# An encoder layer on one core: where the last sums of w_down are sent off, and how long a block waits between its load and its rounding

## The chip, the cores and the metric

The kernel runs on one core of one Trainium2 chip. The metric is the device time of one execution in microseconds; the kernel before takes 1858.98 us in the median of three runs (1856.39 to 1862.3).

## The reference

One transformer-like layer on 512 tokens of width 2048, all in float32:

```
h = RMSNorm(x);  z = h @ w_in            # q, k, v (8 heads of 128) and u (1024)
a = chunked attention(q, k, v)           # relative-position bias, softmax
p = trailing means of u minus u, mixed per group
x = x + RMSNorm(concat(a, p) @ w_o)      # w_o: 2048 x 2048
h = RMSNorm(x)
y = (gelu(conv3(h @ w_up)[:5632]) * conv3(h @ w_up)[5632:]) @ w_down   # w_down: 5632 x 2048
x = x + RMSNorm(y)
```

## The kernel before

**Arithmetic.** Every matrix is split into a rounded part and a rest (`split`, L140 on ScalarE and L141 on VectorE: `hi` is the rounded copy, `lo = src - hi`). A product is three matmuls, hi·hi, hi·lo and lo·hi (`mm3`, L162, L164, L165), each 128x512 in one PSUM bank. Large products are done by a seven-product scheme on 2x2 blocks (numbered 1 to 7, "L" and "a11 ... a22" in the names), so it needs sums of weight blocks as well as blocks.

**Sums of weights in DRAM.** Those sums are made by the DMA engines: `sums_in_dram` (from L285) is a generator of 48 transfers of 1 MB. A `copy` writes a block to a DRAM tile (`wt..` for w_o, `t_108` to `t_115` for the first 1024 rows of w_down), an `add` accumulates another block onto it. 32 are for w_o, 16 for w_down: copy and add to sum 5 (t_108, t_109), sum 7 (t_110, t_111), sum 6 (t_112, t_113, copied from t_108, t_109) and sum 4 (t_114, t_115, copied from t_112, t_113). `more_sums(n)` sends off the next n of them. It is called at places written by hand: in the loop over v (7 times), among the q and k products (18), in the head loop (4), in `mid` (8 over its calls), after `pool_keep` (7), and in `wo_product` (4). As long as `more_sums.paced` is true, a transfer is issued by GpSimd behind a pair of one-column memsets (`pace`: L295 on VectorE behind the last `split`, then L296 on GpSimd), so that it starts when the program has come that far. In w_o it is false: there a copy goes onto SyncE's queue behind the last weight load (L304), an add onto GpSimd's with no pace (L308).

**w_o.** Products run in the order 1, 7, 2, 5, 6, 3, 4, each for two column blocks `cc`, each in four steps `q`. A step reads one weight tile of 0.5 MB (`wo_cc_q` in the order, `wo_q` in the trace): SyncE loads it (L152) into one of 5 `raw` buffers, `split` writes hi and lo into one of 4 pairs of buffers, TensorE uses it for 12 matmuls. I number these tiles from the first of product 7 as T0: eight a product, so T16 is the first of product 5, T21 its sixth, T32 the first of product 3, T40 the first of product 4. Outputs are collected by `copy_out` (L902, ScalarE) and `add_out` (L906, VectorE); after product 6 there are three additions of 128x2048 (L946, L948, L949); after products 3 and 4 a norm, then `x2` (L980), the transposes `xt` back (L995) and their split into `gT` (L143, L144), which the first up-projection (`up`) reads.

**Ready blocks.** In the steps of products 7 to 4 the generator `ready_blocks` (from L839) also prepares three unsummed blocks of w_down as six half blocks: load `rw` (L843, SyncE), wait for some steps, `split` into `rwh` and, in place, `rw`; a step later the stores `rw01h`/`rw01l` and so on (L850, SyncE). There is one buffer of each, so a load waits until the store of the half block before has landed. They are read much later, in the down-projection.

**Who orders what.** TensorE's order is the program's. The other engines' queues are put in order when the program is built, from the order of the code, the buffers and the builder's own estimate of when things are ready. Each queue then runs strictly in that order.

Of the kernel before, what the change touches and what calls it, by code (L numbers as in the profile page):

```python
# [45 lines left out]
def f32(ap):  # L46
    return ap.bitcast(F32)
# [34 lines left out]
def encoder_layer(ctx: ExitStack, tc: tile.TileContext, x, xT, vecs, rel, post_mix, post_ffn,  # L82
# [23 lines left out]
    def bank(name):  # L106
        return psum.tile([P, 512], F32, tag="ps", name=name)
# [30 lines left out]
    def split(hi, lo, src, scale=None):  # L138
        if scale is None:
            rounded = nc.scalar.activation(hi, src, AF.Copy)  # L140
            rest = nc.vector.tensor_sub(lo, src, f32(hi))  # L141
        else:
            rounded = nc.scalar.activation(hi, src, AF.Copy, scale=scale)  # L143
            rest = nc.vector.scalar_tensor_tensor(lo, src, scale, f32(hi), op0=ALU.mult, op1=ALU.subtract)  # L144
        split.last, split.rest = rounded.ins, rest.ins
        return rounded.ins
# [182 lines left out]
    def more_sums(n):  # L329
        for _ in range(n):  # L330
            next(sums_step, None)
# [20 lines left out]
    for kb in range(KD):  # L352
        i, o = divmod(kb, 8)
# [9 lines left out]
        for what in "qk":  # L363
            _, hi, lo = first[f"{what}0_{i}"]
# [14 lines left out]
    def v_steps(i, ps):  # L379
        for n, c in enumerate(VORDER[i]):  # L380
            w = weights.get(f"v{i}_{c}", 2 if (i, n) == (1, 0) else None)
            if not i:
                pairs.prefetch(3 - FIRST_PART + weights.used)
            for j in range(2):
                kb = 2 * c + j
                for t in range(NT):
                    mm3(ps[t], g_tokens(hT, kb, t), part(w, j), n == j == 0, n == 7 and j == 1)
                if j and not i:
                    pairs.prefetch(3 - FIRST_PART + weights.used)
                yield  # L390
# [107 lines left out]
    psv = [bank(f"v0_{t}") for t in range(NT)]  # L498
    sums_of_x = x_sums()
    for n, _ in enumerate(v_steps(0, psv)):  # L500
        if n in (1, 3, 5, 7, 9, 11, 13):
            more_sums(1)
        for _ in range(2):
            next(sums_of_x, None)
        if n == 9:
            for i, v in enumerate(differences):
                split(*(hT[i][:, :, at, :] for at in AT[1]), v)
            early_x.close()
            p0 = mixing_w.enter_context(tc.tile_pool(name="p0", bufs=1, reuse_waits="tile"))
# [103 lines left out]
    with tc.tile_pool(name="p1", bufs=2, reuse_waits="tile") as p1:  # L613
# [43 lines left out]
        def ready_head(h):  # L657
            v = state.pop(("z", h))
            with tc.issue_after(split.rest):
                nc.vector.tensor_mul(v, v, RR)  # L660
            pair = [p1.tile([P, 2, S], F32R, tag="qk" + p, bufs=1, name="qk" + p) for p in "hl"]
            split(*pair, v)
            state["qk", h] = [tuple(p[:, n, :] for p in pair) for n in range(2)]
            if h + 1 < HEADS:
                load_z(h + 1)
# [6 lines left out]
        def v_ready():  # L672
            vh, vl = state["v"]
            for t in range(NT):
                with tc.issue_after(split.last):
                    split(vh[:, t, :], vl[:, t, :], f32(vl)[:, t, :], rt[:, t:t + 1])

        def scores(h):
            (q, k), bias = state.pop(("qk", h)), state.pop(("bias", h))
            with tc.issue_after(split.rest):  # L680
                nc.vector.memset(bias[:CHUNK, S - CHUNK:], -1e30)
            products = [bank(f"s{h}_{t}") for t in range(1, NT)]
            products = [products[0][:, 256:], *products]
            for t in range(NT):
                m = max(2, t + 1) * P
                sl = slice(t * P, (t + 1) * P)
                mm3(products[t][:, :m], (q[0][:, sl], q[1][:, sl]), (k[0][:, :m], k[1][:, :m]), True, True)
            for t in range(NT):
                n, ps = (t + 1) * P, products[t]
                s = t512("s", bufs=4)  # L690
                nc.vector.scalar_tensor_tensor(s[:, :n], ps[:, :n], SCALE, bias[:, S - n:],
                                               op0=ALU.mult, op1=ALU.add)
                nm = p1.tile([P, 1], F32, tag="st", bufs=16, name="nm")
                nc.vector.tensor_reduce(nm, s[:, :n], axis=AX.X, op=ALU.max, negate=True)
                sm = p1.tile([P, 1], F32, tag="st", bufs=16, name="sm")
                nc.scalar.activation(s[:, :n], s[:, :n], AF.Exp, bias=nm, accum_out=sm)
                rs = p1.tile([P, 1], F32, tag="st", bufs=16, name="rs")
                nc.vector.reciprocal(rs, sm)
                nc.vector.tensor_scalar_mul(s[:, :n], s[:, :n], rs)
                state["p", h, t] = s  # L700
            if h + 1 < HEADS:
                load_bias(h + 1)

        def turn(h):
            probs = [state.pop(("p", h, t)) for t in range(NT)]
            pts = [bank(f"pt{h}_{k}") for k in range(3)]
            pts = [pts[0], pts[1][:, P:], pts[2][:, 2 * P:], pts[1][:, :P]]
            for k in (0, 1, 3, 2):
                for t in range(k, NT):
                    nc.tensor.transpose(pts[k][:, (t - k) * P:(t - k + 1) * P],  # L710
                                        probs[t][:, k * P:(k + 1) * P], ident)
            for k in range(NT):
                n, at = S - k * P, PT_AT[k] + k * P - PT_Q[k]
                split(pth[:, at:at + n], ptl[:, at:at + n], pts[k])

        def values(h):
            ps = bank(f"a{h}")
            d = slice((h % 4) * DH, (h % 4 + 1) * DH)
            for k in range(NT):
                sl = slice(PT_AT[k], PT_AT[k] + S - PT_Q[k])  # L720
                mm3(ps[:, PT_Q[k]:], part(state["v"], k, d), (pth[:, sl], ptl[:, sl]), k == 0, k == NT - 1)
            nc.scalar.activation(mix(h), ps, AF.Copy)
# [42 lines left out]
        def run(n):  # L765
            for _ in range(n):
                next(steps, None)

        v_load(0)
        for h in range(3):  # L770
            if not h:
                run(2)
                ready_head(0)
            run(1)
            scores(h)
            if h:
                more_sums(1)
            run(1)
            if h:
                values(h - 1)  # L780
                more_sums(1)
            run(1)
            ready_head(h + 1)
            run(1)
            turn(h)
            if not h:
                v_ready()
# [3 lines left out]
        def mid(h):  # L791
            def step():
                values(h)
                more_sums(2 if h in (3, 4) else 1)
                if h == 2:
                    scores(3)
                elif h + 2 < HEADS:
                    ready_head(h + 2)
                if h == 3:
                    v_load(1)  # L800
            return step
# [37 lines left out]
        def ready_blocks():  # L839
            for at, j in ready_parts:  # L840
                v, hi = (p2.tile([P, 1024], dt, tag=tag, name=tag) for tag, dt in (("rw", F32), ("rwh", F32R)))
                lo = v.bitcast(F32R)
                nc.sync.dma_start(v.rearrange("p (a b) -> p a b", a=2),  # L843
                                  first_block(at[0], at[1] - 1, 0)[:, 2 * j:2 * j + 2, :])
                for _ in range(4):
                    yield
                split(hi, lo, v)
                yield
                for dest, part_ in zip(ready_w[at], (hi, lo)):
                    nc.sync.dma_start(dest[:, 2 * j:2 * j + 2, :], f32(part_).rearrange("p (a b) -> p a b", a=2))  # L850
                for _ in range(2):
                    yield

        ready_steps = ready_blocks()

        def wo_product(i, cc, left, between=None):
            ps = [bank(f"m{i}{cc}{t}") for t in range(2)]
            if cc and i in (2, 5, 6, 3):
                more_sums(1)
            for q in range(4):  # L860
                w = weights.get(f"wo{i}_{cc}_{q}")
                for j in range(2):
                    kb = 2 * q + j
                    for t in range(2):
                        mm3(ps[t], tuple(v[:, kb, t * P:(t + 1) * P] for v in left), part(w, j), kb == 0, kb == 7)
                if i != 1:
                    next(ready_steps, None)
                if between:
                    between(q)
            return ps  # L870
# [877 lines left out]
```

## Time and profile before

| | |
|---|---|
| median of 3 runs | 1858.98 us (1856.39 to 1862.3) |
| the profiled execution's own time | 1859.2 us |
| its span, first to last instruction | 1857.4 us |
| TensorE (PE) busy | 1843.6 us, 99% of the span |
| VectorE (DVE), ScalarE (ACT), GpSimd (POOL) busy | 1540.8, 1082.3, 303.2 us |
| granted TensorE clock | 0.999 |
| v and q/k products | about 30 to 215 us |
| heads and u projections | about 215 to 390 us |
| w_o | about 390 to 550 us |
| up-projection, down-projection | about 550 to 1440, 1440 to 1857 us |

Times are microseconds from the start of the span. A row of the timeline gives start, duration, engine, line, operation, output<-inputs, and in brackets how long the engine had stood idle before it and whom it waited for. A row of the waits gives engine and line, whom it waited for, and then the total, the number and the longest of these waits. "SPq" is SyncE's queue of DMA issues; a DMA's "us to landing" counts from its issue to its last byte. A matmul's duration overlaps with its successor's, so gaps of TensorE are read from the distance of starts.

### The profile page before, as it was taken

What the parts mean: (1) busy time and instruction counts of PE and PEld (TensorE: products, weight loads), DVE (VectorE), ACT (ScalarE), POOL (GpSimd) and SP (SyncE); (2) the same over time, 40 slices, a digit from 0 to 9 for tenths busy, and PEclk for the clock granted to TensorE, in tenths of its full rate; (3) what the DMA queues carried; (4) which work ended last, traced back from release to release, by engine and by line L of the source; (5) the groups of instructions that cost most, each with busy time, mean ns of one, the idle gap of its engine ahead of it and who ended that gap; (6) DMA issues with size and microseconds to landing.
All of it is one profiled execution on the core that took longest, in us unless ns stands there. A gap on an engine that the chain in (4) does not pass through costs nothing.

```text
span 1857.4 us, 25457 instructions
## 1 busy us (share of the span) xinstructions
PE 1843.6 (99%) x9598; PEld 1584.8 (85%) x9598; DVE 1540.8 (83%) x1804; ACT 1082.3 (58%) x1376; POOL 303.2 (16%) x402
## 2 busy tenths in 40 slices
PE   9999999999999999999999999999999999999998
PEld 7888888888878888888888888888888888888886
DVE  6988777887698988888888888888887899899876
ACT  7654455456464666566666665656655655565553
POOL 3411000100000122212222122121121001111101
PEclk9999999999999999999999999999999999999999
DMA  8599978999994798988888888899888967777785
GB/s 319 174 318 297 320 232 236 267 255 331 348 328 144 186 213 195 208 210 195 203 198 206 209 199 198 204 206 202 200 176 293 363 220 175 193 210 178 176 229 159
DMA packets 139338, 426.01 MB, mean 229 GB/s; under 512 B 11920, under 2 KB 15376, under 8 KB 133520
## 3 DMA queue, kind: packets, MB, share of 16 engines
q0 software_dynamic: 54864, 173.56, 46.1%
q1 hardware_dynamic: 84352, 250.84, 38.4%
q8 instruction: 75, 1.23, 0.3%
q14 instruction: 47, 0.39, 0.1%
HBM read 370.35 MB, written 104.33 MB: 256 GB/s over the span
## 4 chain that ended last, share of the span: by engine, by line
PE 93%; DMA 3%; DVE 2%; ACT 1%; issue 1%; SPq 0%; DVEq 0%; POOL 0%; POOLq 0%; ACTq 0%
PE qa L170 18%; PE qa L176 10%; PE qg L170 9%; PE qg L176 5%; PE qd L170 4%; PE pa L164 4%; PE pa L165 4%; PE pa L162 4%; PE qd L176 2%; PE pg L164 2%; PE pg L165 2%; PE pg L162 2%; PE m L164 2%; PE m L165 2%; PE m L162 2%; PE v L164 2%
## 5 line engine op out<-in xcount | busy, mean ns | idle before, releaser
L140 ACT ACTIVATE wfh<-wx 128x1024 fp32r<-128x1024 f32 x192 | 203.4, 1059 | 152.7 <-PE qg L170 55.4
L170 PE MATMUL qa<-gT,wfh 128*128 128x512 f32 x1152 | 288.6, 392 | 0.0
L141 DVE TENSOR_TENSOR wfl<-wx,wfh 128x1024 fp32r<-128x1024 f32 x192 | 234.7, 1222 | 59.8 <-ACT wfh L140 44.8
L170 PEld LDWEIGHTS qa<-gT,wfh 128*128 128x128 f32 x1152 | 207.2, 189 | 37.1
L1365 POOL DMA_DIRECT2D wx<-in_w_up x122 | 104.7, 858 | 502.2 <-DVE wfl L141 473.8
L140 ACT ACTIVATE wfh<-wy 128x1024 fp32r<-128x1024 f32 x96 | 101.7, 1060 | 109.3 <-PE qg L170 57.9
L170 PE MATMUL qg<-h,wfh 128*128 128x512 f32 x656 | 162.2, 389 | 0.9 <-ACT zb L1421 0.9
L176 PE MATMUL qa<-gT,wfl 128*128 128x256 f32 x1152 | 161.2, 283 | 0.1
L176 PEld LDWEIGHTS qa<-gT,wfl 128*128 128x128 f32 x1152 | 151.6, 191 | 4.3 <-ACT zm L1425 0.3
L170 PEld LDWEIGHTS qg<-h,wfh 128*128 128x128 f32 x656 | 122.9, 188 | 26.7 <-ACT zb L1421 1.3
L141 DVE TENSOR_TENSOR bl<-b,bh 128x2048 fp32r<-128x2048 f32 x56 | 127.2, 2287 | 19.1 <-ACT bh L140 11.7
L140 ACT ACTIVATE bh<-b 128x2048 fp32r<-128x2048 f32 x56 | 106.1, 1913 | 55.1 <-DVE b L1129 22.8
L141 DVE TENSOR_TENSOR wfl<-wy,wfh 128x1024 fp32r<-128x1024 f32 x96 | 117.2, 1221 | 10.9 <-ACT wfh L140 6.4
L162 PE MATMUL pa<-bh,ah 128*128 128x512 f32 x320 | 124.5, 389 | 0.0
L164 PE MATMUL pa<-bl,ah 128*128 128x512 f32 x320 | 124.5, 389 | 0.0
L165 PE MATMUL pa<-bh,al 128*128 128x512 f32 x320 | 124.5, 389 | 0.0
L141 DVE TENSOR_TENSOR wfl<-wz,wfh 128x1024 fp32r<-128x1024 f32 x48 | 58.7, 1224 | 54.1 <-PE qa L170 54.1
L176 PEld LDWEIGHTS qg<-h,wfl 128*128 128x128 f32 x656 | 89.5, 190 | 6.4
L170 PE MATMUL qd<-gT,wfh 128*128 128x512 f32 x384 | 94.9, 389 | 0.0
L176 PE MATMUL qg<-h,wfl 128*128 128x256 f32 x656 | 91.5, 282 | 0.0
L170 PEld LDWEIGHTS qd<-gT,wfh 128*128 128x128 f32 x384 | 72.0, 188 | 14.9
L170 PE MATMUL qa<-h,wfh 128*128 128x512 f32 x328 | 82.1, 392 | 0.0
(550 smaller groups left out, 4363.5 us busy)
## 6 DMA issues: line engine op xcount, KB each, us to landing
wx<-in_w_up POOLq DMA_DIRECT2D x122, 512.0 KB, 6.1
b<-in_w_down SPq DMA_DIRECT2D x32, 1024.0 KB, 6.8
wt<-in_w_o POOLq DMA_DIRECT2D x24, 1024.0 KB, 15.8
wx<-in_w_up SPq DMA_DIRECT2D x43, 512.0 KB, 5.5
wz<-in_w_up SPq DMA_DIRECT2D x41, 512.0 KB, 6.0
wy<-in_w_up SPq DMA_DIRECT2D x41, 512.0 KB, 4.6
wy<-in_w_up POOLq DMA_DIRECT2D x41, 512.0 KB, 6.9
sum<-part POOLq DMA_DIRECT2D x38, 512.0 KB, 6.8
```

What stands on the lines that cost most here:

```text
L140: rounded = nc.scalar.activation(hi, src, AF.Copy)
L141: rest = nc.vector.tensor_sub(lo, src, f32(hi))
L162: nc.tensor.matmul(ps, l[0], r[0], start=first, stop=False, skip_group_check=onto)
L164: nc.tensor.matmul(low, l[0], r[1], start=False, stop=False, skip_group_check=onto)
L165: nc.tensor.matmul(ps, l[1], r[0], start=False, stop=last, skip_group_check=onto)
L170: nc.tensor.matmul(ps, w[0][:, kb], pairs[kb][0], start=fresh and not kb, stop=last, skip_group_check=not fresh)
L176: nc.tensor.matmul(ps[:, sl], w[1][:, kb], pair[:, sl], start=False, stop=last, skip_group_check=not fresh)
L1365: nc.gpsimd.dma_start(self.raw[k, what], self.block(k, m, kh), accum_op=ALU.add)
```

## The change

The number of transfers stays 48, and so does their order. Three calls of `more_sums` are added early and three are taken out of `wo_product`: the v loop calls it 8 times (also at its last step), the head loop also at head 0, `mid` twice also at head 5; `wo_product` calls it at product 5 only. The last four transfers, the copies and adds of sum 4, so become three paced ones and one in w_o. In `ready_blocks` five steps instead of four lie between load and split, and one instead of two behind the stores, so a half block still takes seven steps.

```diff
     for n, _ in enumerate(v_steps(0, psv)):
-        if n in (1, 3, 5, 7, 9, 11, 13):
+        if n % 2:
             more_sums(1)
...
             scores(h)
-            if h:
-                more_sums(1)
+            more_sums(1)
...
                 values(h)
-                more_sums(2 if h in (3, 4) else 1)
+                more_sums(2 if h in (3, 4, 5) else 1)
...
-                for _ in range(4):
+                for _ in range(5):
                     yield
                 split(hi, lo, v)
                 yield
                 for dest, part_ in zip(ready_w[at], (hi, lo)):
                     nc.sync.dma_start(dest[:, 2 * j:2 * j + 2, :], f32(part_).rearrange("p (a b) -> p a b", a=2))
-                for _ in range(2):
-                    yield
+                yield
...
-            if cc and i in (2, 5, 6, 3):
+            if cc and i == 5:
                 more_sums(1)
```

What this does to the queues shows at three places. The first is GpSimd's queue from the end of the heads to the first norm of w_o; `t_114` and `t_115` are sum 4, `small` is the norm's power. Before:

```order
L308 DMA t_112<-in_w_down 512x1x512
L296 MEMSET pace 128x1
L308 DMA t_113<-in_w_down 512x1x512
L308 DMA t_114<-in_w_down 512x1x512
L308 DMA t_115<-in_w_down 512x1x512
L967 TENSOR_TENSOR small<-small,mhalf 128x2 x2
```

In the change:

```order
L308 DMA t_113<-in_w_down 512x1x512
L296 MEMSET pace 128x1
L301 DMA t_114<-t_112 16x16384
L296 MEMSET pace 128x1
L301 DMA t_115<-t_113 16x16384
L308 DMA t_115<-in_w_down 512x1x512
L296 MEMSET pace 128x1
L308 DMA t_114<-in_w_down 512x1x512
L965 TENSOR_TENSOR small<-small,mhalf 128x2 x2
```

Both copies now stand in GpSimd's queue, paced, and the add onto t_115, though written in product 5, needs no pace and stands ahead of the last paced one.

The second is SyncE's queue in w_o from the second half block's store to the third and fourth loads; `wt_96` and `wt_97` hold the weights of product 5, `wo_0_1r` there is T17. Before:

```order
L850 DMA rw01l<-rw 128x1024
L152 DMA wo_0_1r<-wt_96 128x1024
L304 DMA t_114<-t_112 16x16384
L152 DMA wo_0_2r<-wt_96 128x1024
L152 DMA wo_0_3r<-wt_96 128x1024
L152 DMA wo_1_0r<-wt_97 128x1024
L843 DMA rw<-in_w_down 128x2x512
L152 DMA wo_1_1r<-wt_97 128x1024
L152 DMA wo_1_2r<-wt_97 128x1024
L152 DMA wo_1_3r<-wt_97 128x1024
L850 DMA rw11h<-rwh 128x1024
```

In the change:

```order
L849 DMA rw01l<-rw 128x1024
L152 DMA wo_0_1r<-wt_96 128x1024
L152 DMA wo_0_2r<-wt_96 128x1024
L842 DMA rw<-in_w_down 128x2x512
L152 DMA wo_0_3r<-wt_96 128x1024
L152 DMA wo_1_0r<-wt_97 128x1024
L849 DMA rw11h<-rwh 128x1024
L849 DMA rw11l<-rw 128x1024
L152 DMA wo_1_1r<-wt_97 128x1024
L152 DMA wo_1_2r<-wt_97 128x1024
L152 DMA wo_1_3r<-wt_97 128x1024
L842 DMA rw<-in_w_down 128x2x512
```

The copy is gone, the third load stands behind T18's instead of T20's, and the fourth, which before stood behind T27's, behind T23's: five tiles between the two loads instead of seven. The fifth moves from behind T34's to behind T30's, the sixth from behind T40's to behind T37's.

The third is ScalarE's queue in product 5; `wo_0_0h` there is T16, `wo_1_1h` T21, `junk` sums of squares. Before:

```order
L140 ACTIVATE wo_0_0h<-wo_0_0r 128x1024
L140 ACTIVATE wo_0_1h<-wo_0_1r 128x1024
L140 ACTIVATE wo_0_2h<-wo_0_2r 128x1024
L140 ACTIVATE rwh<-rw 128x1024
L140 ACTIVATE wo_0_3h<-wo_0_3r 128x1024
L910 ACTIVATE junk,small<-y_4299 128x1024
L140 ACTIVATE wo_1_0h<-wo_1_0r 128x1024
L910 ACTIVATE junk,small<-y_4299 128x1024
L140 ACTIVATE wo_1_1h<-wo_1_1r 128x1024
```

In the change:

```order
L140 ACTIVATE rwh<-rw 128x1024
L140 ACTIVATE wo_0_0h<-wo_0_0r 128x1024
L140 ACTIVATE wo_0_1h<-wo_0_1r 128x1024
L140 ACTIVATE wo_0_2h<-wo_0_2r 128x1024
L140 ACTIVATE wo_0_3h<-wo_0_3r 128x1024
L908 ACTIVATE junk,small<-y_4311 128x1024 x2
L140 ACTIVATE wo_1_0h<-wo_1_0r 128x1024
L140 ACTIVATE rwh<-rw 128x1024
L140 ACTIVATE wo_1_1h<-wo_1_1r 128x1024
```

The third rounding moves ahead of T16, and the fourth, which stood behind T25, ahead of T21; the fifth moves from behind T32 to behind T27, the sixth from behind T40 to behind T34. VectorE's subtractions `rw<-rw,rwh` move with them: the last one leaves its place among the tiles of product 4 and comes to stand in product 3, just ahead of T35.

## The prediction

> **What bounds the kernel now.** I read the page's first table, then TensorE's waits, then its starts one by one.
>
> ```profile
> span 1857.4 us, 25457 instructions
> PE 1843.6 (99%) x9598; PEld 1584.8 (85%) x9598; DVE 1540.8 (83%) x1804; ACT 1082.3 (58%) x1376; POOL 303.2 (16%) x402
> ```
>
> TensorE is busy 1843.6 of 1857.4 us, and the change leaves its instructions and their order as they are. So only its gaps can shrink, and a wait anywhere else matters only if it opens a new one. The waits of TensorE (engine and line, waited for, total, times, longest):
>
> ```profile
> PE up L162 <- DVE gT L144: 1.6, 1, 1.6
> PE up L164 <- DVE gT L144: 0.7, 2, 0.5
> PE m L164 <- DVE wo_1l L141: 0.3, 1, 0.3
> PE m L164 <- DVE wo_0l L141: 0.3, 1, 0.3
> ```
>
> All of these lie in w_o (`m`) or just behind it (`up` waits for `gT`); the few others are at the program's start and in the up-projection, which the change does not touch. The recorded idle time understates a gap, as the starts show:
>
> ```profile
> 509.61 0.39 PE L162 MATMUL m<-wo_3h,s 128*128 128x512 f32 x1
> 510.07 0.50 PE L164 MATMUL m<-wo_3l,s 128*128 128x512 f32 x1
> 512.74 0.39 PE L162 MATMUL m<-wo_0h,s 128*128 128x512 f32 x1
> 513.41 0.50 PE L164 MATMUL m<-wo_0l,s 128*128 128x512 f32 x1 [0.28 <-DVE wo_0l L141]
> 516.04 0.39 PE L162 MATMUL m<-wo_1h,s 128*128 128x512 f32 x1
> 516.75 0.50 PE L164 MATMUL m<-wo_1l,s 128*128 128x512 f32 x1 [0.32 <-DVE wo_1l L141]
> ```
>
> Undisturbed, starts are 0.23 us apart (two rows further down, 458.06 and 471.66, stand five tiles of 12 matmuls apart: 2.72 us a tile). These three steps take 0.46, 0.67 and 0.71, together 1.15 too long, and the late matmuls last 0.50 instead of 0.39, which holds up the next ones by 0.11 each: 1.5 us lost. With the 1.6 and the 0.7 above, w_o and its end hold 3.8 us that a better order could give back, 0.2% of the span. That caps the gain.
>
> Why VectorE is late with those tiles: first the chain of waits (start, duration, what), then ScalarE's timeline.
>
> ```profile
> 463.05 8.42 DMA rw11l<-rw
> 483.14 10.00 DMA rw11l<-rw
> ```
>
> ```profile
> 500.77 1.06 ACT L140 ACTIVATE rwh<-rw 128x1024 fp32r<-128x1024 f32 x1 [5.22 <-DMA rw<-in_w_down]
> ```
>
> A half block's load waits for the store before it, SyncE's queue waits with it, and ScalarE stands 5.22 us before a load that has not landed, with VectorE's subtraction behind it and the w_o tiles behind that. VectorE does not catch up before the norm. Transfers are slow there, since the DMA engines are full. The queues and issues of the window from 440 to 495 (for a queue packets, MB, share; for an issue count, KB, median us to landing):
>
> ```profile
> q1 hardware_dynamic: 4638, 17.08, 81.5%
> q0 software_dynamic: 1056, 2.10, 20.6%
> t<-in_w_down POOLq DMA_DIRECT2D x2, 1024.0 KB, 15.9
> rw<-in_w_down SPq DMA_DIRECT2D x3, 512.0 KB, 7.5
> rw11l<-rw SPq DMA_DIRECT2D x2, 512.0 KB, 9.2
> rw01l<-rw SPq DMA_DIRECT2D x1, 512.0 KB, 3.9
> ```
>
> The last two adds are all of q0's 20.6%, the two copies of 1 MB about a tenth of what q1 moved, so some 10%.
>
> **The change part by part.** *The four transfers leave w_o.* This frees about 30% of the DMA engines from 440 to 495 and two issues from SyncE's queue. The add written in product 5 stands in GpSimd's queue right behind a copy that is issued among the heads, so it goes early too.
>
> *The half blocks come closer together*, load to load 5 tiles (13.6 us at 2.72 a tile) instead of 7 for the third and fourth. With L for a load and S for a store of the rest:
>
> ```profile
> 434.45 0.37 SPq L843 DMA_DIRECT2D rw<-in_w_down  x1
> 440.43 1.06 ACT L140 ACTIVATE rwh<-rw 128x1024 fp32r<-128x1024 f32 x1 [2.81 <-issue]
> 442.78 0.32 SPq L850 DMA_DIRECT2D rw01l<-rw  x1
> 447.32 0.34 SPq L152 DMA_DIRECT2D wo_2r<-wt  x1
> 458.06 0.39 PE L164 MATMUL m<-wo_0l,n 128*128 128x512 f32 x1
> 471.66 0.39 PE L164 MATMUL m<-wo_1l,n 128*128 128x512 f32 x1
> ```
>
> The third load now follows T18's (447.32), so it goes at 448. Behind its landing come rounding (1.1), its subtraction (1.15) and the subtraction of T16, which now stands behind it (1.2): T16 is ready at 451.5 + L, and TensorE reads it at 458.06. The store goes at 448 + L + 2.3, the fourth load at 448 + L + 2.3 + S + 0.4, and T21, behind its rounding, is ready at 454.2 + 2L + S; TensorE reads it at 471.66. So T16 needs L up to 6.6, T21 needs 2L + S up to 17.5. The second load gives L = 6.0 (434.45 to 440.43). S was 3.9 as the first copy began, 9.2 beside copies and adds, and for the last two stores of the phase, from the page's list of DMA issues:
>
> ```profile
> rw02l<-rw SPq DMA_DIRECT2D x2, 512.0 KB, 5.9
> ```
>
> I take L = 6.0 and S from 3.9 to 5.9, the rows with fewer sums beside them: 2L + S is 15.9 to 17.9, T21 0 to 0.4 us late; I count 0.4. With 7.5 and 9.2 it is the rival A below. The fifth and sixth loads follow at seven tiles (19 us) each, and the cycle L + S + 2.7 is 14.6 at most: nothing.
>
> *What then happens at 500 to 570.* Without the 5.22 us for which the tiles stood behind a load, the three come in time: -1.5. And the norm's chain comes earlier:
>
> ```profile
> 526.82 1.22 DVE L141 TENSOR_TENSOR rw<-rw,rwh 128x1024 fp32r<-128x1024 f32 x1
> 527.96 0.68 DVE L906 TENSOR_TENSOR y<-m,y 128x512 f32<-128x512 f32 x1
> ```
>
> Product 3 ended on TensorE at 524.6 (471.66, 19 more tiles, the 1.5 lost, less a matmul). Its output is added 3.3 us later, since VectorE is behind and does the sixth `rw` (1.2) first. That one moves into product 3, and the backlog goes with the stall. The norm's chain runs on VectorE from there to `gT`; 3.3 us earlier there cover the 1.6 us wait even with TensorE 1.5 us earlier: -1.6. The two smaller waits for `gT` (0.7) hang on product 4's end, which moves up as TensorE does: counted at 0, at best -0.7.
>
> *Three more paced transfers among v and the heads.* Each costs VectorE a one-column memset in phases where TensorE waits for nothing, and GpSimd a memset and an issue, 0.8 us by the distance of two adds. GpSimd's only other work near them is the power for the first norm, which comes to stand behind the transfer added at the end of v:
>
> ```profile
> 77.43 1.82 POOL L308 DMA_DIRECT2D wt<-in_w_o  x1
> 78.22 2.32 POOL L308 DMA_DIRECT2D wt<-in_w_o  x1
> 79.99 1.63 POOL L218 TENSOR_TENSOR rt<-rt,mhalf 128x4 f32<-128x4 f32 x1
> 82.33 0.60 PE L223 MATMUL R<-ident,rt 128*128 128x128 f32 x4
> ```
>
> It ends at 81.62, TensorE needs it at 82.33: 0.7 us of cover for 0.8 of delay, so 0.1, dropped as rounding. The thin place is the end of the heads. The last paced slot is
>
> ```profile
> 386.26 1.16 POOL L308 DMA_DIRECT2D t<-in_w_down  x1
> ```
>
> and in the change the slots before it carry the two copies, and this one both last adds. Here the first w_o tiles are loaded (ScalarE, VectorE, TensorE; then the loads' time to landing in the window 380 to 420):
>
> ```profile
> 402.39 1.06 ACT L140 ACTIVATE wo_2h<-wo_2r 128x1024 fp32r<-128x1024 f32 x1 [4.68 <-DMA wo_2r<-in_w_o]
> 403.48 1.23 DVE L141 TENSOR_TENSOR wo_2l<-wo_2r,wo_2h 128x1024 fp32r<-128x1024 f32 x1 [2.01 <-ACT wo_2h L140]
> 406.38 0.39 PE L164 MATMUL m<-wo_2l,a 128*128 128x512 f32 x1
> ```
>
> ```profile
> wo_1r<-in_w_o SPq DMA_DIRECT2D x1, 512.0 KB, 15.0
> wo_2r<-in_w_o SPq DMA_DIRECT2D x1, 512.0 KB, 10.5
> ```
>
> This tile is ready at 404.71 and read at 406.38: 1.67 us of slack. Its load took 10.5 us while one add ran. The nearest row for a worse case is the tile before it, which took 15.0 us: 4.5 later, less 1.67, is +2.8. From below, two copies in place of two adds could bring it earlier, but no gap is there to close: 0. I take 0, since its load already ran beside an add all the way.
>
> A sentence of the Trainium skill bears on this: DMA: Bandwidth & Descriptors, "Queues, rings and completion order", says that each DMA engine goes round robin over the queues that have work, a packet at a time. By it a second add in GpSimd's queue keeps that queue busy for longer but takes no more than its half from SyncE's loads, so the price would be 0. No run here shows one add against two beside the same load.
>
> Sum: -1.5 - 1.6 + 0.4 = -2.7, on the profiled execution's own 1859.2 us (span 1857.4 and 1.8 around it), which stands 0.2 above the median of the runs: **1856.5 us**.
>
> **The rivals.** *A: the ready blocks become the wait.* If L and S stay as they were (7.5 and 9.2), because w_o's own loads fill the engines, T16 is 0.9 late and 2L + S = 24.2 puts T21 6.7 late in all. Against the -3.1 that is +3.6: 1862.8. It decides from 2L + S = 20.6. For it: three of the six half blocks now come sooner and stand further ahead of the tiles; against it: the 3.9 us store. *B: the heads pay.* The +2.8 above eats the gain: 1859.3. For it: 1.67 us of slack, and the same bytes moved to where the DMA engines are also busy; against it: TensorE waited for no tile there, although this load was among the slowest. The Trainium skill says on the same page, "Issuing engines are not separate DMA queues", that a transfer runs on the same 16 engines whichever queue issues it; the 15.0 us row agrees, and it is what B rests on. *C: the relief does nothing*, VectorE stays behind through its own work (the three 128x2048 additions): 1859.2. *A and B together*: 1862.8 + 2.8 = 1865.6.
>
> **How the numbers follow.** Forecast 0.50, B 0.18, C 0.09, A 0.17, A with B 0.06. The forecast's best, with the 0.7 and the 0.4 back, is 1855.4. Single runs of before lie from 1856.39 to 1862.3, 3 us to either side, so I put 2 us below that, 1853.5, and on top 1864.0, a little over A; A with B is left out. About 0.3% (5.6 us) is what a measurement of this kernel tells from no change. Faster by more, under 1853.4, needs more than the gaps hold: 0.05. Slower by more, over 1864.6, is A with B and A's upper part: 0.12. Within: 0.83.
>
> **What would show it.** Right: no TensorE wait for `wo_.l` between 500 and 520, `up` no longer waiting 1.6 us for `gT`, `rw11l` landing in under 6 us, and the third and fourth `rwh` waiting under 5 us for their loads. Wrong: gaps at T16 or T21 (near 458 and 471), which is A; a gap between 400 and 415, which is B; or both gaps at 510 and 550 as before, C.

## The result, and the profile after

The changed kernel takes 1866.97 us (median of 5 runs, 1865.08 to 1867.78), the kernel before 1858.49 beside it (1856.39 to 1862.3): a ratio of 1.0049, with a 95% interval from 1.0038 to 1.006. It is 8.5 us slower. The prediction was 1856.5 us, with a range up to 1864.0: the sign was wrong, and the time lies above the range. The profiled execution took 1866.97 us.

The first table of its page, and TensorE's waits up to 700 us, without those at the program's start and in the first projections (engine and line, waited for, total, times, longest):

```profile
span 1865.2 us, 25457 instructions
...
PE 1847.0 (99%) x9598; PEld 1586.2 (85%) x9598; DVE 1540.2 (83%) x1807; ACT 1082.6 (58%) x1376; POOL 304.4 (16%) x407
```

```profile
PE u L162 <- DVE ptl L141: 2.3, 1, 2.3
PE up L162 <- DVE gT L144: 2.0, 1, 2.0
PE m L164 <- DVE wo_0l L141: 1.3, 2, 0.9
...
PE R L223 <- POOL rt L218: 0.9, 1, 0.9
PE m L164 <- DVE wo_3l L141: 0.6, 1, 0.6
PE m L164 <- DVE wo_2l L141: 0.3, 1, 0.3
PE m L164 <- DVE wo_1l L141: 0.3, 1, 0.3
...
```

Two waits are new and lie far ahead of w_o: `u` for `ptl` (among the heads, near 318 us) and the `R` transposes for `rt` (near 82). Both waits in w_o that should have gone are there still: the late tiles (now four, T35 to T38, near 517 to 527) and `up` for `gT`, 2.0 instead of 1.6. A third is new in w_o, `wo_0l` at T16:

```profile
464.78 0.50 PE L164 MATMUL m<-wo_0l,n 128*128 128x512 f32 x1 [0.94 <-DVE wo_0l L141]
```

**The first new wait.** GpSimd's queue at the end of v, and TensorE's row behind it:

```profile
77.93 2.33 POOL L308 DMA_DIRECT2D wt<-in_w_o  x1
78.67 1.69 POOL L296 MEMSET pace<- 128x1 f32 x1
78.71 2.84 POOL L308 DMA_DIRECT2D wt<-in_w_o  x1
79.70 3.36 POOL L218 TENSOR_TENSOR rt<-rt,mhalf 128x4 f32<-128x4 f32 x1
```

```profile
83.11 0.65 PE L223 MATMUL R<-ident,rt 128*128 128x128 f32 x4 [0.91 <-POOL rt L218]
```

The power for the first norm ends at 83.06 instead of 81.62. The adds start 0.8 us apart, but they end at 80.26 and 81.55, 1.3 apart. What follows an add ends behind it, as the rows show: the memset between the two ends at 80.36, 0.1 us behind the first add, and the power 1.5 us behind the second (in the kernel before 1.1 us behind its last add).

**The second new wait.** ScalarE stands before the rounding of the second half of v, whose load `vl<-vd` has not landed:

```profile
314.08 2.56 ACT L143 ACTIVATE vh<-vl,rt 128x512 fp32r<-128x512 f32 x4 [7.12 <-DMA vl<-vd]
```

The same in the kernel before, then the DMA issues from 295 to 325 us of before and after (count, KB, median us to landing):

```profile
310.56 2.56 ACT L143 ACTIVATE vh<-vl,rt 128x512 fp32r<-128x512 f32 x4 [4.43 <-DMA vl<-vd]
```

```profile
t<-in_w_down POOLq DMA_DIRECT2D x2, 1024.0 KB, 18.4
wt<-in_w_o POOLq DMA_DIRECT2D x1, 1024.0 KB, 14.3
vl<-vd SPq DMA_DIRECT2D x1, 1024.0 KB, 6.8
```

```profile
t<-in_w_down POOLq DMA_DIRECT2D x3, 1024.0 KB, 16.8
vl<-vd SPq DMA_DIRECT2D x1, 1024.0 KB, 9.5
```

The load takes 9.5 us instead of 6.8. Everything behind it on ScalarE and VectorE comes later: `pth`, `ptl`, the rounding of `u_0`. There are as many transfers beside it as before, but with two calls added ahead of this place, others: the kernel before issues an add and two copies there, the changed one a copy and two adds.

**In w_o** the transfers do go. From 440 to 495 us only SyncE's queue is left, and loads and stores land faster (`rw` in 5.5 us instead of 7.5, `rw11l` in 5.8 instead of 9.2):

```profile
q1 hardware_dynamic: 5351, 16.80, 87.4%
rw<-in_w_down SPq DMA_DIRECT2D x4, 512.0 KB, 5.5
rw11l<-rw SPq DMA_DIRECT2D x2, 512.0 KB, 5.8
```

Yet ScalarE waits longer for the half blocks than before. Its third, fifth and sixth `rwh`:

```profile
461.27 1.06 ACT L140 ACTIVATE rwh<-rw 128x1024 fp32r<-128x1024 f32 x1 [6.87 <-issue]
...
494.02 1.06 ACT L140 ACTIVATE rwh<-rw 128x1024 fp32r<-128x1024 f32 x1 [6.02 <-DMA rw<-in_w_down]
...
513.92 1.06 ACT L140 ACTIVATE rwh<-rw 128x1024 fp32r<-128x1024 f32 x1 [7.29 <-DMA rw<-in_w_down]
```

VectorE's subtraction behind the fourth rounding (474.29) and SyncE's queue from there to the fifth load show why:

```profile
477.47 1.22 DVE L141 TENSOR_TENSOR rw<-rw,rwh 128x1024 fp32r<-128x1024 f32 x1
...
479.85 0.32 SPq L152 DMA_DIRECT2D wo_3r<-wt  x1
480.22 0.43 SPq L849 DMA_DIRECT2D rw11h<-rwh  x1
...
481.36 0.96 SPq L849 DMA_DIRECT2D rw11l<-rw  x1
...
489.87 0.38 SPq L842 DMA_DIRECT2D rw<-in_w_down  x1
```

The rest's store goes out 7.1 us after its rounding began, not the 2.3 that the two engines need. VectorE subtracts a weight tile first, T21, so the half block's subtraction ends 4.4 us behind the start of the rounding. Then the store stands 2.7 us in SyncE's queue, behind weight loads that wait for a free buffer. It lands 8.5 us later, the next load 4.2 after that: 19.7 us from rounding to rounding, and 19.9 to the one after. The seven tiles of a block give 19.0. So each half block comes 0.7 to 0.9 us later against its tiles, and the last one meets T35.

**The sum.** For each kernel I added up by how much two neighbouring starts in TensorE's timeline stand farther apart than undisturbed (0.227 us for a matmul of 512 columns, 0.120 for 256, others in proportion). It is one profiled execution each, a missing record adds 0.2, and fixed gaps such as those of transposes are in it too; so only differences of over half a microsecond in a cell are read. "w_o" is 400 to 600 us and ends with `up`. A stretch in which TensorE runs at half its clock (last section) adds about 1.5 us to a cell. Such a stretch lies in 300-340 of the change, of "no call at v's end" and of the change with held loads, in w_o of the change, of "no call at v's end" and of both kernels with late calls, and in 200-300 of both with sums in q, k. The time is the median, with the ratio to the kernel before on the same chip and its 95% interval; one execution of "sums in q, k (1)" that took 3747 us is left out, and so is one of the kernel before beside it, of 10581 us.

| kernel | 60-100 | 200-300 | 300-340 | 340-400 | w_o | us | ratio |
|---|---|---|---|---|---|---|---|
| before | 1.0 | 2.2 | 1.3 | 1.2 | 8.1 | 1858.5 | 1 |
| the change | 2.2 | 2.4 | 5.5 | 1.2 | 11.9 | 1867.0 | 1.0049 [1.0038, 1.006] |
| steps only | 1.1 | 2.2 | 1.6 | 1.2 | 8.0 | 1859.6 | 1.0007 [0.9994, 1.0019] |
| moves only | 2.1 | 2.4 | 3.7 | 2.2 | 10.0 | 1865.5 | 1.0039 [1.0025, 1.0053] |
| no call at v's end | 0.8 | 2.2 | 6.0 | 1.3 | 10.8 | 1866.2 | 1.0044 [1.0031, 1.0057] |
| late calls | 0.8 | 2.4 | 1.4 | 1.7 | 14.5 | 1866.3 | 1.0047 [1.0031, 1.0063] |
| left out | 1.0 | 2.2 | 1.4 | 1.2 | 9.1 | 1862.0 | 1.0012 [1.0002, 1.0022] |
| left out, loads held | 1.0 | 2.2 | 1.5 | 2.6 | 4.6 | 1856.0 | 0.9985 [0.9976, 0.9995] |
| before, loads held | 0.8 | 2.9 | 1.3 | 2.7 | 6.9 | 1858.4 | 1.0002 [0.9991, 1.0013] |
| the change, loads held | 2.3 | 2.4 | 5.3 | 1.4 | 4.3 | 1860.0 | 1.0007 [0.9997, 1.0016] |
| vl beside one copy | 1.8 | 2.2 | 3.1 | 1.2 | 12.6 | 1866.7 | 1.0037 [1.0023, 1.0051] |
| late calls, loads held | 0.8 | 2.4 | 1.3 | 1.2 | 11.7 | 1861.0 | 1.0011 [1.0001, 1.002] |
| no sum by vl, held | 2.0 | 2.4 | 1.3 | 1.2 | 8.6 | 1860.9 | 1.0011 [1.0002, 1.002] |
| and rt first | 0.8 | 2.5 | 1.3 | 1.2 | 7.8 | 1858.8 | 0.9996 [0.9986, 1.0006] |
| add first, held | 1.1 | 3.3 | 2.3 | 5.1 | 4.2 | 1862.2 | 1.0023 [1.0013, 1.0033] |
| sums in q, k (1) | 1.1 | 10.9 | 1.8 | 1.3 | 4.1 | 1864.3 | 1.004 [1.0027, 1.0052] |
| sums in q, k (2) | 1.0 | 12.1 | 1.8 | 1.3 | 6.1 | 1865.3 | 1.0041 [1.0029, 1.0053] |

The change costs 1.2 at `rt`, 4.2 at `ptl` and 3.8 in w_o, 9.2 in all; about 1.5 each of the last two is half clock, behind the waits for `ptl` and for `gT`. Elsewhere some 1.4 come back, for the spans of the two profiled executions differ by 7.8; the medians differ by 8.5.

### The profile page after: what moved, and what is told of

The parts are those of the page before. It is cut to its first block, busy times and chain, and to the rows that moved or that the text cites. A ratio compares the mean times of both kernels' runs of the same rounds, so it can differ in the third digit from the quotient of the medians.

```text
span 1865.2 us, 25457 instructions
## 1 busy us (share of the span) xinstructions
PE 1847.0 (99%) x9598; PEld 1586.2 (85%) x9598; DVE 1540.2 (83%) x1807; ACT 1082.6 (58%) x1376; POOL 304.4 (16%) x407
## 4 chain that ended last, share of the span: by engine, by line
PE 90%; DVE 3%; DMA 3%; issue 1%; ACT 1%; POOL 1%; SPq 0%; DVEq 0%; POOLq 0%; ACTq 0%
PE qa L170 18%; PE qa L176 10%; PE qg L170 9%; PE qg L176 5%; PE qd L170 4%; PE pa L165 4%; PE pa L164 4%; PE pa L162 4%; PE qd L176 2%; PE pg L165 2%; PE pg L164 2%; PE pg L162 2%; PE u L162 2%; PE u L164 1%; PE u L165 1%
## 5 line engine op out<-in xcount | busy, mean ns | idle before, releaser
L141 DVE TENSOR_TENSOR bl<-b,bh 128x2048 fp32r<-128x2048 f32 x56 | 127.1, 2286 | 18.5 <-ACT bh L140 11.7
L162 PE MATMUL pa<-bh,ah 128*128 128x512 f32 x320 | 124.5, 389 | 0.0
```

The source lines that it names most:

```text
L162: nc.tensor.matmul(ps, l[0], r[0], start=first, stop=False, skip_group_check=onto)
```

## The experiments

The first theory, P, put the loss where the transfers had been moved to. Its rival S blamed the half blocks' steps.

**The steps alone, and the moves alone.** The kernel before with 5 and 1 steps, and the changed one with 4 and 2:

```diff
-                for _ in range(4):
+                for _ in range(5):
                     yield
                 split(hi, lo, v)
...
-                for _ in range(2):
-                    yield
+                yield
```

> The kernel before with the five steps of the ready blocks alone; all 48 transfers stand where they stood. Theory P (the loss stands where the moved transfers stand: about 1.2 us at the R transposes near 81 us and about 4.8 us between 300 and 340 us, the rest, about 2.5 us, in w_o): no loss before 440 us, 1858 to 1862 us, so at most 3.5 us over the kernel before. Theory S (the steps are the change's cost: a block's load goes out one tile after its write instead of two and SyncE stands before it): 1864 us or more. In both the excess of TensorE between 300 and 340 us stays near the 1.3 us of before.

> The changed kernel with the ready blocks' steps put back to four and two; only the transfers are moved. Theory P: the R wait near 81 us (0.9 us) and the wait of u for ptl near 318 us (2.3 us) both stay, 1863 to 1867 us. Theory S: 1858 to 1861 us, with the two early waits worth nothing.

1859.62 us for the steps, 1865.49 for the moves, with the waits for `rt` and `ptl` (0.8 and 2.1 us) in the latter. S has fallen: the interval of the steps alone holds 1, and in the queues they move no rounding at all. With the steps of before, but the transfers gone, the roundings stand on ScalarE just where the changed kernel has them. So it is the missing transfers in w_o, not the steps, that move the half blocks ahead. On top of the moves the steps add 1.5 us by the medians, but the two intervals overlap, so that stays open. Of the table's differences (5.5 against 3.7, 11.9 against 10.0) about 1.5 each is half clock, which the profiled execution of the moves alone does not have.

**Other places for the calls.** One kernel without the call at v's end (made at product 3 instead), and one with all three at heads 5, 6 and 7:

```diff
-        if n % 2:
+        if n in (1, 3, 5, 7, 9, 11, 13):
...
-            if cc and i == 5:
+            if cc and i in (5, 3):
```

```diff
-        if n % 2:
+        if n in (1, 3, 5, 7, 9, 11, 13):
...
-            more_sums(1)
+            if h:
+                more_sums(1)
...
-                more_sums(2 if h in (3, 4, 5) else 1)
+                more_sums(2 if h >= 3 else 1)
```

> The changed kernel without the call at the last step of v; that transfer is made in w_o, at product 3. Every call up to head 5 shifts by one less. Theory P: the 0.9 us wait of the R transposes for rt goes (1.2 us of the time); whether the vl stall at 318 us stays hangs on which two transfers stand beside vl's load now (two copies as before, so it should shrink from 2.3 us toward the 0.6 us of before): 1860 to 1865 us. Theory S: 1866 to 1868 us, no change.

> The changed kernel with the three transfers put at heads 5, 6 and 7 (one more each) instead of the last step of v, head 0 and head 5; every transfer before 325 us stands where it stood before the change, and w_o keeps its one. Theory P: the waits near 81 us and 318 us are those of before (0 and about 1.3 us of excess), w_o is as in the changed kernel: 1859 to 1862 us. Theory S, and a theory that any three transfers more among the heads cost TensorE the same wherever they stand: 1865 to 1868 us.

1866.18 and 1866.30 us. In the first the wait for `rt` is gone, as P said, but `ptl`'s grew to 2.9 us: with one shift less, two copies start ahead of vl's load. In the second both early waits are gone, and still nothing is won, since w_o now loses 14.5 instead of 11.9. P's list of places was too short: w_o itself had to be taken apart. Both times also fit the rival by which any three transfers more among the heads cost the same wherever they stand. Against it speak the places of the gaps, and the times below: with held loads they run from 1858.8 to 1865.3 us by the places of the calls. TensorE's waits in the late calls between 400 and 480 us:

```profile
PE m L164 <- DVE wo_0l L141: 2.5, 3, 1.0
PE m L164 <- DVE wo_3l L141: 0.8, 1, 0.8
```

**Relief and order in w_o, apart.** Theory O: with the transfers gone the half blocks move ahead of the tiles, and that costs more than the relief gives. Rival H: w_o is worse only because the heads hand over late. In "left out" the four transfers of w_o are not made at all and none is added elsewhere:

```diff
-            if cc and i in (2, 5, 6, 3):
-                more_sums(1)
...
-        source = first_sum[i][cc] if i in first_sum else ...
+        source = first_sum[6 if i == 4 else i][cc] if i in first_sum else ...
```

To put the half blocks back without a transfer, their loads are held behind the newest weight load. This is done to the changed kernel, to the one with the transfers left out, and as a control to the kernel before:

```diff
-                nc.sync.dma_start(v.rearrange("p (a b) -> p a b", a=2), ...)
+                with tc.issue_after(load_w.last):
+                    nc.sync.dma_start(v.rearrange("p (a b) -> p a b", a=2), ...)
```

> The kernel before with the four transfers of w_o (sum 4) not made at all and none added elsewhere; the reader of sum 4 takes sum 6, so this part of the result is left out. The steps are those of before, but with the transfers gone the half blocks' loads and roundings move ahead by themselves, to where the changed kernel has them. Theory O (w_o loses by that order, and the DMA relief does not pay for it): 1859 to 1861.5 us, with a wait for wo_0l near 458 us and gT's wait at 2.0 us instead of 1.6. Theory H (w_o is only worse in the changed kernel because the heads hand over late, the relief itself works): 1855 to 1857.5 us.

> The changed kernel with each half block's load issued behind the newest load of a weight, which puts the third, fourth and sixth rounding on ScalarE back to the places of before and the fifth within a tile of it, with w_o as empty of transfers as in the changed kernel. Theory O: no wait for wo_0l near 463 us, the late tiles near 517 us gone or halved, gT's wait not above 1.6: 1862.5 to 1865.5 us, with the early waits (81 and 318 us) unchanged. Theory H: 1866 to 1868 us, w_o's waits as in the changed kernel.

> The kernel before without the four transfers of w_o (sum 4 left out, its reader takes sum 6) and with the half blocks' loads held as in the run of the changed kernel with held loads: what w_o would give with the transfers gone and the order of before. Theory O: the late tiles at 510 us and part of gT's wait go: 1855 to 1857.5 us, 1 to 3.5 us under the kernel before. If the late tiles and gT's wait come from VectorE's own work, 1858 to 1860 us, no gain even so.

> The control for the hold: the kernel before, all transfers in their places, with the half blocks' loads held. The queues' order is that of before but for the sixth load, one tile later. If the gain of the run with sum 4 left out and the loads held came from the empty DMA engines: 1857.5 to 1859.5 us, the late tiles at 510 us stay. If it came from the hold itself: 1855.5 to 1857 us, and the late tiles are gone here too.

The relief alone makes the kernel slower, by 0.12% (1861.95 us; 1.0 more in w_o, `gT` at 2.0). The hold alone does nothing to the time (1858.42): by its row 1.2 us less in w_o stand against 1.5 more in 340-400 and 0.7 more in 200-300. Both together win 2.7 us (1855.96), as O said; H has fallen. In the changed kernel the hold takes 7 us off (1860.04), more than the 1.5 to 4.5 that O expected. O was wrong in one point: with the transfers left out T16 does not wait, so that wait needs the later load of the changed kernel too. TensorE's waits from 400 to 600 us, first the longest with the transfers left out, then all of the change with held loads:

```profile
PE up L162 <- DVE gT L144: 2.0, 1, 2.0
...
```

```profile
PE up L164 <- DVE gT L144: 0.2, 1, 0.2
```

All of the 3.8 us that the prediction saw in w_o come back, and the reason stands in ScalarE's last three `rwh` with held loads. They wait 2.75, 2.02 and nothing, where the changed kernel's last two wait 6 and 7 us:

```profile
482.77 1.06 ACT L140 ACTIVATE rwh<-rw 128x1024 fp32r<-128x1024 f32 x1 [2.75 <-DMA rw<-in_w_down]
498.37 1.06 ACT L140 ACTIVATE rwh<-rw 128x1024 fp32r<-128x1024 f32 x1 [2.02 <-DMA rw<-in_w_down]
521.35 1.04 ACT L140 ACTIVATE rwh<-rw 128x1024 fp32r<-128x1024 f32 x1
```

**What delays vl.** The changed kernel with two of the three transfers beside vl's load made later (one copy stays), and, with held loads, all three made later:

```diff
-                more_sums(2 if h in (3, 4, 5) else 1)
+                more_sums({3: 0, 4: 4, 5: 2}.get(h, 1))
```

```diff
-                more_sums(2 if h in (3, 4, 5) else 1)
+                more_sums({3: 0, 4: 5, 5: 2}.get(h, 1))
...
-                more_sums(1)
+                more_sums(int(j != 1))
```

> The changed kernel with the two transfers of head 3 made at head 4, so that vl's load goes out beside one copy instead of a copy and two adds. If the adds beside vl's load are the cause of the wait at 318 us: ptl's wait falls from 2.3 us to under 0.5, the slow matmuls behind it go, and the time falls by 3 to 5 us to 1862 to 1864, unless the four transfers at head 4 open a wait near 330 to 345 us. If ScalarE's and VectorE's own queues make ptl late: the wait stays above 1.5 us and the time at 1866 to 1868 us.

> The changed kernel with held loads, and with no transfer beside vl's load: those of the step before it and of head 3 are made at head 4, five in a row. If the copy that starts right ahead of vl's load is what makes vl late (9.5 us to landing beside a copy first, 6.8 beside an add first): vl lands in 7 us or less, ptl's wait is under 0.5 us, the slow matmuls behind it go, and the time is 3 to 4.5 us under the 1860.0 of the changed kernel with held loads: 1855.5 to 1857.5 us. If vl's load is slow by itself: the wait stays above 1.2 us, 1859 to 1861 us.

With one copy the load takes 8.7 us and `ptl`'s wait is 1.5, not under 0.5, so most of the delay is the copy's and not the adds'. Without any transfer the load takes 4.7 us and the wait is gone:

```profile
vl<-vd SPq DMA_DIRECT2D x1, 1024.0 KB, 4.7
```

```profile
309.07 2.56 ACT L143 ACTIVATE vh<-vl,rt 128x512 fp32r<-128x512 f32 x4 [2.76 <-DMA vl<-vd]
```

That settles the cause, the transfers beside the load. The wait follows the load's time to landing from kernel to kernel: 0.8 us at 8.0, 1.5 at 8.7, 2.1 at 9.3, 2.3 at 9.5 and 2.9 at 10.1, always 7.2 less, and none at 6.8 and 4.7. So the kernel before, at 6.8, had 0.4 us to spare. It does not settle the time: 1866.70 and 1860.92 us. What was put off ends later, and w_o's first tiles wait: 3.8 and 3.9 us of gaps between 400 and 480 us, where the kernel before has none.

**rt, and late calls with held loads.** The call at v's end made behind the first norm (on top of the last kernel), and the late calls with held loads:

```diff
-        if n % 2:
+        if n in (1, 3, 5, 7, 9, 11, 13):
...
             spread1()
+            more_sums(1)
```

> As the run with no transfer beside vl's load, and the transfer added at v's last step is called behind the first norm instead. If GpSimd's power stood behind that add: the wait of the R transposes for rt (1.1 us) goes and the time falls by 1 to 1.5 us against the run before it, to 1854.5 to 1856.5 us, under the kernel before by 2 to 4. If not: no change against it.

> The three transfers at heads 5, 6 and 7 (as in the run with late calls) and the half blocks' loads held behind the newest weight load. Theory O (the half blocks' places in the queues cost w_o what the run with late calls lost): the waits at 449 and 461 us and gT's 2.0 us go, what is left is at most the two tiles near 434 and 438 us (1.7 us): 1855.5 to 1859.5 us. If the late transfers themselves make w_o's first loads late whatever the order: waits for wo_3l and wo_0l at 430 to 465 us stay, 1862 to 1866 us.

Without the added transfer ahead of it the power ends in time and the wait for `rt` is gone, for 2.1 us by the medians (1858.82, where only 1.2 of TensorE's gaps went). The total missed what was expected by 2 us, because of the tiles near 434 to 450 that I had not counted for the kernel it builds on. The late calls with held loads, 1861.04 us, also miss: the hold won 5 us, but 6.2 us of gaps stay between 400 and 480 us, where I had counted 1.7. There the last adds go out at 405 us instead of 391 and w_o's first loads run beside them. That is rival B's mechanism: 0.7 us fall on B's own place (`wo_2l`, at 407), the rest near 436. Its waits from 400 to 480, and of the issues from 390 to 450 an add and the slowest load:

```profile
PE m L162 <- ACT wo_3h L140: 1.8, 1, 1.8
PE m L164 <- DVE wo_3l L141: 0.8, 1, 0.8
PE m L164 <- DVE wo_2l L141: 0.7, 1, 0.7
```

```profile
t<-in_w_down POOLq DMA_DIRECT2D x2, 1024.0 KB, 19.0
...
wo_0r<-wt SPq DMA_DIRECT2D x3, 512.0 KB, 10.1
```

**Is there a free place?** Three more, all with held loads and the call behind the norm. One has the extra transfer of head 5 at head 2, so that vl's load meets an add, an add and a copy; two keep all transfers away from vl's load by making three more among the q and k projections (the second has `i == 2 and k in (3, 4, 5)` in the same place):

```diff
-                more_sums(2 if h in (3, 4, 5) else 1)
+                more_sums(2 if h in (2, 3, 4) else 1)
```

```diff
-        if i in (3, 7, 4) and k < pairs.n - 1:
+        if (i in (3, 7, 4) or i == 1 and k in (1, 2, 3)) and k < pairs.n - 1:
...
-                more_sums(2 if h in (3, 4, 5) else 1)
+                more_sums({3: 0, 4: 2, 5: 2}.get(h, 1))
...
-                more_sums(1)
+                more_sums(int(j != 1))
```

> The changed kernel with held loads, the transfer of v's last step called behind the first norm, and the extra one of head 5 given to head 2 instead, before vl's load: one more transfer has gone by then, so that vl's load meets an add, an add and a copy in that order (as many as in the kernel before, which has an add and two copies there) and not a copy first. If the kind that stands first decides: vl lands in about 7 us, ptl's wait is gone (under 0.5 us), no wait for rt, and since the sums end earlier among the heads no tile of w_o is late between 430 and 450 us: 1854.5 to 1857 us, 1.5 to 4 us under the kernel before. If the number of transfers near vl's load decides: vl lands in 8.5 us or more, ptl's wait is 1.5 us or more, 1858.5 to 1861 us.

> As the run with rt first and no transfer beside vl's load, but the three transfers kept away from vl's load are made earlier, one at each of products (1,1), (2,1) and (3,1) of the q and k projections, not later in head 4. If every wait so far came from its place (rt behind an add, vl beside a copy, w_o's first tiles beside adds that end late, the half blocks moved ahead), all four are gone: the last adds go out near 391 us as in the changed kernel and no tile of w_o waits: 1855 to 1857 us, 1.5 to 3.5 under the kernel before. If the projections pay (a wait of qa, qg or qd for a factor): 1858 to 1861 us.

> The same with the three transfers at products (3,2), (4,2) and (5,2) of the q and k projections. Same expectations: 1855 to 1857 us if the places of the waits are all of it, 1858 to 1861 us if the projections pay.

1862.17, 1864.29 and 1865.29 us: no. With the adds first vl's load takes 8.0 us and `ptl` waits 0.8, between the two expectations, so neither kind nor number alone decides, and how they share stays open. That kernel loses its gain to a wait of `s` for `qkh` (2.5 us, up to 349). In the projections w_o is clean, but the first heads pay 8.7 and 9.9 us. TensorE's waits of the first of the two from 200 to 300, and its slowest loads from 205 to 260:

```profile
PE pt L711 <- DVE s L700: 2.3, 3, 1.7
PE s L162 <- DVE ptl L141: 1.5, 1, 1.5
PE s L162 <- ACT qkh L140: 1.1, 1, 1.1
...
```

```profile
q0 software_dynamic: 2662, 8.34, 59.7%
vl<-vd SPq DMA_DIRECT2D x1, 1024.0 KB, 20.7
v_3r<-in_w_v SPq DMA_DIRECT2D x1, 512.0 KB, 22.6
```

The same vl load of that stretch took 8.2 us in the changed kernel. No kernel that makes all 48 transfers was faster than the one before.

## Why the prediction was wrong

- **"Phases where TensorE waits for nothing"**: this failed first and cost 5.4 us. That TensorE waits for nothing says that the slack has been enough so far, not how much there is. I asked it of one tile at the end of the heads, found 1.67 us, and put the other added transfers at nothing. vl's load had hardly any: it landed 2.7 us later and TensorE waited 2.3. The added calls did not even bring more transfers to it, they shifted the list so that another kind stood there. The kernels in which one or both of these waits went when the calls were moved show that the place was the cause. Behind the wait for `ptl`, and behind the 2.0 us for `gT`, half clock added about 1.5 us each, for which the sum had no term.
- **The power for `rt`**, "0.1, dropped": right mechanism, wrong size. I took the distance of two adds' starts, 0.8. The rows quoted for it give their ends too, 79.25 and 80.54, 1.3 apart, and the power ends behind the last of them. That makes 0.6 of the wait of 0.9; the rest is that the power ended 1.5 us behind the last add instead of 1.1, and why stays open.
- **T16, "needs L up to 6.6"**: L was 6.4 (the load was issued at 454.90, the rounding began at 461.27), so size and formula were right: 454.90 + 3.5 + 6.4 is 464.8, and TensorE read T16's rest at 464.78. But the load was issued 1.4 us later against T16 than I took it, so that L could be 5.2 at most: 1.2 us late. T21, for which I counted 0.4, did not wait.
- **"The cycle L + S + 2.7 is 14.6 at most: nothing"** failed. Of the 2.7 us, 2.3 were the two engines' time from rounding to the store's issue. That took 7.1, since the half block stands behind a weight tile on VectorE and behind weight loads in SyncE's queue, and S was 8.5. With that the cycle is 19.7 against 19.0, and so the late tiles stay, now T35 to T38. It is rival A one turn later than A had it. That the half blocks' place ahead of the tiles is the cause, the runs with held loads show; that it works by this cycle is read from the rows, and how much the 0.7 us a block adds is not shown apart.
- **"-1.5" and "-1.6"** did not come, since both rest on the half blocks landing in time. The terms themselves were sound: with the order mended, w_o gives 3.5 us with the transfers left out (8.1 to 4.6) and 3.8 in the changed kernel; the time of the former, 2.7 us under before, is the predicted sum, in part by luck: 1.4 of the 3.5 us are lost again in 340-400, as in the control.
- **The relief** was right in the profile (5.5 and 5.8 us to landing) and wrong as a cause: alone it costs.
- **B** did not show in the changed kernel, and that is no merit of the 0 in the sum. The tile's load took 13.2 us instead of 10.5, but TensorE, held up by the two earlier waits, read the tile 5.0 us later than in the kernel before, which left 3.0 us of slack. Whether it would have waited without them, no run shows. B's mechanism did show at vl, and at B's own place once the calls went later.
- **C**, that VectorE stays behind through its own work, has fallen: with the transfers gone and the loads held the three additions are still there, and neither a late tile nor the wait of `up` L162 for `gT` is left.
- The Trainium skill's sentence from DMA: Bandwidth & Descriptors, "Queues, rings and completion order", that an engine goes round robin between queues, fits vl's load: 4.7 us alone, 8.7 beside one copy, a bit more than half speed. The 6.8 us beside an add and two copies do not follow from it. My use of it was at fault: I asked what a second transfer takes at one place, and not what another kind of transfer does at the other places.

## What to carry to other kernels

A transfer that leaves a crowded stage has a price where it goes, and the price hangs on the load with the least slack there, not on how busy TensorE looks; before such a move, list for each load near the new places when it lands and when its tile is read. A list of work that several places draw from shifts everywhere behind an added call, so look at what each later place now gets. And where a scheduler sets the queues, taking work out can move other work ahead: here that order cost more than the relief gave, and one line that held the loads back won 7 us.

## What the runs showed of the hardware

Behind the wait for `ptl` TensorE ran at half its clock for 3.4 us. The rows of the changed kernel, and the granted clock of a stretch (the column behind POOL's):

```profile
318.23 0.66 PE L162 MATMUL u<-gT,u_0h 128*128 128x512 f32 x1 [2.31 <-DVE ptl L141]
...
321.68 0.46 PE L165 MATMUL u<-gT,u_0l 128*128 128x512 f32 x1
321.98 0.40 PE L162 MATMUL u<-gT,u_0h 128*128 128x512 f32 x1
```

```profile
318.00:320.00 2.00, 1.77 (x5) 1.39 (x6) 2.00 (x4) 2.00 (x4) 0.00 (x0) 0.60 1.14 227
```

Starts stand 0.43 us apart instead of 0.23 up to 321.68. That made 4.2 us out of a wait of 2.3. The same came behind the 2.02 us for `gT`, where starts stand 0.21 us apart instead of 0.12 up to 564.1:

```profile
562.00:564.00 2.00, 2.00 (x11) 2.00 (x11) 1.96 (x4) 2.00 (x6) 0.00 (x0) 0.50 0.96 383
```

The length of the wait alone does not decide. In the late calls with held loads a wait of 1.78 us, with one of 0.76 a microsecond behind it, was enough, and in the first kernel with sums in q, k waits of 1.08 and 0.88 us, 0.4 us apart. With the moves only, waits of 2.14 and 2.01 us were not, nor was this one in the kernel with the add first, whose clock behind it stays at 1.00:

```profile
349.17 0.39 PE L162 MATMUL s<-qkh 128*128 128x256 f32 x1 [2.51 <-ACT qkh L140]
```

```profile
350.00:352.00 2.00, 1.57 (x10) 1.53 (x11) 1.97 (x5) 1.20 (x4) 0.00 (x0) 1.00 1.09 198
```

What decides, these traces do not show, and it differs between executions of one kernel: of the nine with the add first, those with a mean clock of 0.999 took 1858.2 to 1860.8 us, those with 0.997 took 1862.6 to 1864.4. The Trainium skill, TensorE: Matmul & The Clock Gate, "Part 1: The HAM clock gate", has the half clock and a return after about 3.4 us, and the trace agrees; it puts the fall behind an idle window of about 3.4 us, and here 2.31 us and less were enough.
